# Block products' weights that begin 144 instead of 192 bytes behind their tile's begin

## The chip, the core and the metric

One core of one Trainium2 chip runs the whole kernel, one decoder layer over 512 tokens, in one launch. The metric is device time in microseconds. Before the change three runs took 1109.86, 1110.81 and 1111.26 us, a median of 1110.81 us.

## What is computed

The layer has three stages in a row: a SwiGLU feed-forward network (FFN) at half weight, a token mixer (two kinds of attention), and a second FFN at half weight. Each is normalised before and after. Only the FFNs are touched here. Cut to what matters:

```python
def swiglu(x, w_gate, w_up, w_down):
    return (jax.nn.silu(x @ w_gate) * (x @ w_up)) @ w_down

h = rms_norm(x, ffn1_pre[l])
x = x + 0.5 * rms_norm(swiglu(h, ffn1_w_gate[l], ffn1_w_up[l], ffn1_w_down[l]), ffn1_post[l])
# token mixer
h = rms_norm(x, ffn2_pre[l])
x = x + 0.5 * rms_norm(swiglu(h, ffn2_w_gate[l], ffn2_w_up[l], ffn2_w_down[l]), ffn2_post[l])
```

`x` is 512 by 1024, `w_gate` and `w_up` are 1024 by 2816, `w_down` is 2816 by 1024, all float32.

## The kernel before

**Precision.** Every float32 operand is split into a high and a low part of type `float32r`: ACT casts the high part (`split`, L384), DVE subtracts it from the source for the low part (L391). A product is then three matmuls (`mm3`): high weights by high data (L413), high weights by low data (L414), low weights by high data (L415). In the profile's rows the moving operand stands first and the weights second: `pb_S<-xh_t,whi` streams `xh_t` past the weights `whi`. The weights of a matmul are loaded by an LDWEIGHTS of its own (PEld in the profile), which runs while the matmul before it streams.

**Weight tiles.** `wpair` takes a pair of tiles, `whi` and `wlo`, each 1088 elements (4352 bytes) in every partition, from a pool of three each. A weight block uses 1024 of them; the argument `shift` says how many elements behind the tile's begin they start. Only `block`, in `ffn`, gives a shift, namely `SHIFT`; all other callers leave it at 0.

**Block products.** Both FFNs take their gate and up products for pairs of 128-column groups by a Strassen scheme, `strassen(p)`: for the first FFN with p from 2 to 10, for the second with p from 1 to 10, so 19 times. One call builds seven weight blocks with `block`, from loaded weights (`raw`) or from DVE sums of them (`tmp_t`), and calls `product` seven times. A `product` is 2 column groups by 4 slices of the contraction by 3 matmuls, 24 matmuls. So there are 7 x 24 = 168 matmuls in a call and 19 x 168 = 3192 in the kernel: 1512 in the first FFN and 1680 in the second. Each has weights of 128 by 128 and a moving operand of 128 by 256: a half of `xh`/`xl` or one of the precomputed token sums in `NN`, `N`, `PT` and `CB` tiles.

**Other products.** The first groups of each FFN (`classical`) and the projections of the mixer use unshifted weight tiles. Those with 256 moving columns are the nearest kin of the block products: the matmuls just ahead of the second FFN's first block product stream the same `xh_t` and `xl_t`, 256 columns, past weights that begin at their tile's begin.

**Addresses.** In the built program all these tiles begin at a byte address that leaves 32 when divided by 128: `whi` and `wlo` at 80800, 85152, 89504, 93856, 98208 and 102560, `xh_t` at 34208, `xl_t` at 50592, and so on. A weight slice of a block begins a multiple of 512 bytes behind its block's begin, a moving slice of 256 columns a multiple of 1024 bytes behind its tile's begin. So, counted within stretches of 128 bytes, every moving operand of these products begins at byte 32, unshifted weights at byte 32, and the block products' weights at byte 96 (32 + 192 = 224 = 128 + 96).

**Order.** The order of the instructions on PE, ACT and DVE is written out in a table (`ORDER`). Neither the order nor a single operation depends on `SHIFT`.

Of the kernel before, what the change touches and what calls it, by code (L numbers as in the profile page):

```python
# [294 lines left out]
            8: ["of"] * 2 + ["V"] * 2, 9: ["KB"] * 4}  # L295
STEPS = (2, 2, 2), (4, 2)
EARLY = 5
SHIFT = 48
HOLD_TAGS = ["W"] * 2 + ["Q"] * 4 + ["KA"] * 2 + ["V"] * 2 + ["CB", "ring"]
PS_BUFS = dict(S=3, T=2, V=1, F=2)  # L300
PS_TAGS = [t for t in PS_BUFS for _ in range(PS_BUFS[t])]
# [7 lines left out]
class Layer:  # L309
# [264 lines left out]
    def ffn(self, n, wg, wu, wd, post, finish, xsrc, tags, nps, aside=None):  # L574
# [37 lines left out]
        def block(src):  # L612

            return self.wsplit(src, [4, 2 * P], None, SHIFT)

# [1294 lines left out]
```

## Time and profile before

| what | us |
|---|---|
| median of three runs | 1110.81 |
| the profiled execution's own time | 1109.86 |
| its span, first to last instruction | 1107.8 |
| around the span | 2.06 |
| first FFN's block products on PE, 59.40 to 237.47 | 178.07 |
| second FFN's block products on PE, 799.12 to 996.54 | 197.42 |

All rows come from one profiled execution. A matmul row's duration covers its whole way through the array, so neighbouring matmuls overlap and the busy time of PE says little about its rate; how fast the array works is seen from the distance between the starts of matmuls that follow each other. The timeline shows those starts to 0.01 us, and over a long stretch the distance comes out to a fraction of a nanosecond.

### The profile page before, as it was taken

The numbers are of one execution on the slowest core, as the hardware profiler recorded it, in microseconds if no ns is written. First come the engines' busy times: TensorE is split into PE (matmuls) and PEld (weight loads), VectorE is DVE, ScalarE is ACT, GpSimd is POOL, SyncE is SP. The second block draws the span as 40 slices with busy tenths as digits, with TensorE's granted clock in tenths as the row PEclk, the third lists the DMA queues.
The fourth block names the chain that finished last, engine by engine and source line by source line (L and its number), as shares of the span: only waits on it lengthen the run. The fifth ranks groups of instructions, "written<-read, shape, count | busy, mean of one in ns | idle before, by whom it ended". The sixth has DMA issues, their size and how long they took to land.

```text
span 1107.8 us, 18832 instructions
## 1 busy us (share of the span) xinstructions
PE 1098.6 (99%) x7070; PEld 996.2 (90%) x7070; DVE 915.5 (83%) x1569; ACT 654.2 (59%) x1185; POOL 79.1 (7%) x112
## 2 busy tenths in 40 slices
PE   9999999999999999999999999999999999999997
PEld 7899999998889988888888998888999999998886
DVE  7799999988787878987666687977898888979674
ACT  6455555566564778787565625645565555558562
POOL 1000000000012022443000000001000000000001
PEclk9999999999999999999999999999999999999999
DMA  9967775788964562202567768683324434267862
GB/s 293 308 199 245 225 228 181 222 289 281 317 203 119 165 168 86 84 22 62 169 217 252 236 181 294 220 292 105 103 89 129 129 122 130 92 196 232 294 221 83
DMA packets 153951, 207.36 MB, mean 187 GB/s; under 512 B 19938, under 2 KB 98562, under 8 KB 153604
## 3 DMA queue, kind: packets, MB, share of 16 engines
q1 hardware_dynamic: 153856, 206.16, 57.5%
q8 instruction: 55, 0.90, 0.3%
q14 instruction: 36, 0.29, 0.1%
q10 hardware_dynamic: 4, 0.00, 0.0%
HBM read 166.76 MB, written 39.37 MB: 186 GB/s over the span
## 4 chain that ended last, share of the span: by engine, by line
PE 92%; DVE 3%; DMA 2%; ACT 1%; issue 1%; POOL 0%; SPq 0%; DVEq 0%; POOLq 0%; ACTq 0%
PE pb_F L413 12%; PE pb_F L415 12%; PE pb_F L414 11%; PE pb_S L415 8%; PE pb_S L413 8%; PE pb_S L414 8%; PE pb_T L415 6%; PE pb_T L413 6%; PE pb_T L414 6%; PE pb_V L413 3%; PE pb_V L415 3%; PE pb_V L414 3%; PE pb_V L1344 2%; PE pb_T L1329 2%; PE pb_S L1063 1%; PE pb_S L1064 1%
## 5 line engine op out<-in xcount | busy, mean ns | idle before, releaser
L384 ACT CAST whi<-raw 128x1024 fp32r<-128x1024 f32 (+1 forms) x213 | 217.5, 1023 | 238.2 <-issue 70.2
L391 DVE TENSOR_TENSOR wlo<-raw,whi 128x1024 fp32r<-128x1024 f32 (+1 forms) x213 | 252.5, 1188 | 91.5 <-ACT whi L384 87.2
L413 PE MATMUL pb_F<-xh_t,whi 128*128 128x512 f32 (+1 forms) x392 | 141.7, 363 | 0.1
L415 PE MATMUL pb_F<-xh_t,wlo 128*128 128x512 f32 (+1 forms) x392 | 140.9, 362 | 0.2 <-DVE wlo L391 0.2
L414 PE MATMUL pb_F<-xl_t,whi 128*128 128x512 f32 (+1 forms) x392 | 140.5, 360 | 0.0
L384 ACT CAST whi<-tmp_t 128x1024 fp32r<-128x1024 f32 x58 | 60.8, 1049 | 55.9 <-PE pb_S L414 22.2
L391 DVE TENSOR_TENSOR wlo<-tmp_t,whi 128x1024 fp32r<-128x1024 f32 x58 | 70.9, 1222 | 16.9 <-ACT whi L384 16.6
L415 PEld LDWEIGHTS pb_F<-xh_t,wlo 128*128 128x128 f32 x392 | 73.9, 188 | 9.5 <-DVE wlo L391 0.6
L413 PEld LDWEIGHTS pb_F<-xh_t,whi 128*128 128x128 f32 x392 | 73.9, 188 | 9.5 <-issue 0.3
L414 PEld LDWEIGHTS pb_F<-xl_t,whi 128*128 128x128 f32 x392 | 73.9, 189 | 8.9
L413 PE MATMUL pb_S<-xh_t,whi 128*128 128x256 f32 (+1 forms) x232 | 66.9, 288 | 0.0
L415 PE MATMUL pb_S<-xh_t,wlo 128*128 128x256 f32 (+1 forms) x232 | 66.7, 288 | 0.0
L414 PE MATMUL pb_S<-xl_t,whi 128*128 128x256 f32 (+1 forms) x232 | 66.6, 287 | 0.0
L1320 POOL TENSOR_SCALAR SP_s<-SP_s,st_t 128x384 f32<-128x384 f32 (+2 forms) x48 | 49.6, 1051 | 100.0 <-DVE wlo L391 50.5
L435 POOL TENSOR_TENSOR rs_t<-rs_t,mhalf_t 128x1 f32<-128x1 f32 x24 | 15.6, 648 | 532.2 <-DVE rs_t L431 531.7
L413 PE MATMUL pb_T<-xh_t,whi 128*128 128x256 f32 x184 | 51.2, 283 | 0.6 <-DVE xl_t L496 0.6
L415 PE MATMUL pb_T<-xh_t,wlo 128*128 128x256 f32 x184 | 51.6, 283 | 0.0
L414 PE MATMUL pb_T<-xl_t,whi 128*128 128x256 f32 x184 | 51.0, 281 | 0.0
L391 DVE TENSOR_TENSOR PT_s<-pb_T,PT_s 128x512 fp32r<-128x512 f32 (+1 forms) x72 | 39.7, 559 | 6.1 <-ACT PT_s L384 5.4
L1069 DVE CUSTOM_DVE_ANT_0 SP_s<-pb_S,W_s 128x128 f32<-128x128 f32 (+2 forms) x92 | 38.6, 443 | 7.1 <-PE pb_S L1064 4.7
L415 PEld LDWEIGHTS pb_S<-xh_t,wlo 128*128 128x128 f32 x232 | 43.7, 188 | 0.6
L414 PEld LDWEIGHTS pb_S<-xl_t,whi 128*128 128x128 f32 x232 | 43.6, 188 | 0.6
(858 smaller groups left out, 3458.6 us busy)
## 6 DMA issues: line engine op xcount, KB each, us to landing
raw<-in_ffn_w_up_dram SPq DMA_DIRECT2D x40, 512.0 KB, 4.5
raw<-in_ffn_w_gate_dram SPq DMA_DIRECT2D x39, 512.0 KB, 4.9
raw<-in_w_in_dram SPq DMA_DIRECT2D x18, 1024.0 KB, 5.6
raw<-in_ffn_w_down_dram SPq DMA_DIRECT2D x14, 1024.0 KB, 5.7
raw<-tdram SPq DMA_DIRECT2D x14, 1024.0 KB, 5.2
NN_s<-in_ffn_w_down_dram SPq DMA_DIRECT2D x22, 512.0 KB, 4.6
tdram<-NN_s SPq DMA_DIRECT2D x22, 512.0 KB, 3.8
odram<-ring_s SPq DMA_DIRECT2D x38, 128.0 KB, 3.5
```

The lines of the kernel that those rows point to most:

```text
L384: self.last_cast = self.nc.scalar.copy(dsthi, src).ins
L391: self.last_rest = self.nc.vector.tensor_sub(dstlo, src, dsthi.bitcast(F32)).ins
L413: mm(out, lhi, rhi, start=start, stop=False, skip_group_check=skip)
L414: mm(out, lhi, rlo, start=False, stop=False, skip_group_check=skip)
L415: mm(out, llo, rhi, start=False, stop=stop, skip_group_check=skip)
L435: nc.gpsimd.tensor_tensor(out=r, in0=v, in1=self.mhalf, op=OP.pow)
L1063: mm(out, q[:, qc], ka[:, kc], start=True, stop=False)
L1064: mm(out, q[:, qc], kb[half][:, kc], start=False, stop=True)
L1069: nc.vector.tensor_tensor_reduce(p, s, w, -1.0, FLOOR, OP.add, OP.min, st_m)
L1320: nc.gpsimd.tensor_scalar(pp, pp, st[:, 1, t:t + 1], None, op0=OP.mult)
L1329: nc.tensor.transpose(b[:, o + (t - kk) * P:o + (t - kk + 1) * P], pt[pn][:, po + kk * P:po + (kk + 1) * P], self.ident)
L1344: self.nc.tensor.matmul(out[:, kk * P:S], v, pp, start=first and kk == 0 and pi == 0, stop=False, skip_group_check=True)
```

## The change

One constant is changed.

```diff
@@ -295,7 +295,7 @@
 STEPS = (2, 2, 2), (4, 2)
 EARLY = 5
-SHIFT = 48
+SHIFT = 36
 HOLD_TAGS = ["W"] * 2 + ["Q"] * 4 + ["KA"] * 2 + ["V"] * 2 + ["CB", "ring"]
```

It is used in one place, L614, and reaches the tiles in `wpair`:

```python
        def block(src):
            return self.wsplit(src, [4, 2 * P], None, SHIFT)
...
            w = self.tile(self.pool, [P, 1088], F32R, tag, tag, 3)[:, shift:shift + n]
```

The high and the low part of each of the 133 weight blocks (19 x 7) now begin 36 elements, 144 bytes, behind the tile's begin. ACT writes the high part there, DVE reads it and writes the low part there, and LDWEIGHTS reads both from there. Within stretches of 128 bytes the block products' weights now begin at byte 48 (32 + 144 = 176 = 128 + 48) instead of byte 96. The tiles, their addresses and sizes, the DMAs, the waits and the order of instructions on each engine stay as they were.

## The prediction

> **What bounds the kernel now.** The page comes first, then PE's waits, then the starts of the matmuls in the block products. From the page:
>
> ```profile
> span 1107.8 us, 18832 instructions
> PE 1098.6 (99%) x7070; PEld 996.2 (90%) x7070; DVE 915.5 (83%) x1569; ACT 654.2 (59%) x1185; POOL 79.1 (7%) x112
> PEclk9999999999999999999999999999999999999999
> PE 92%; DVE 3%; DMA 2%; ACT 1%; issue 1%; POOL 0%; SPq 0%; DVEq 0%; POOLq 0%; ACTq 0%
> ```
>
> PE is busy from end to end at full granted clock, and the chain that ended last is 92% PE. The whole list of PE's waits says the same:
>
> ```profile
> PE pb_V L1798 <- POOL ident_t masks.py:199: 1.5, 1, 1.5
> PE pb_T L413 <- DVE xl_t L496: 0.6, 2, 0.4
> PE pb_S L489 <- DVE tmp_t L484: 0.4, 1, 0.4
> PE pb_F L415 <- DVE wlo L391: 0.2, 1, 0.2
> ```
>
> 2.7 us in all, hardly any in the FFNs. So the time is the number of matmuls by the distance between their starts. Nothing changes the number; the question is whether the address changes the distance. The timeline of PE gives it. Here are the first block product of each FFN and the first matmul behind the last one:
>
> ```profile
> 59.40 0.28 PE L413 MATMUL pb_T<-xh_t,whi 128*128 128x256 f32 x1
> ...
> 237.47 0.40 PE L413 MATMUL pb_F<-whi,Q_s 128*128 128x512 f32 x1
> ...
> 799.12 0.28 PE L413 MATMUL pb_V<-xh_t,whi 128*128 128x256 f32 x1
> ...
> 996.54 0.40 PE L413 MATMUL pb_F<-whi,Q_s 128*128 128x512 f32 x1
> ```
>
> The first FFN's 1512 block matmuls take 237.47 - 59.40 = 178.07 us, 117.8 ns each. The second's 1680 take 996.54 - 799.12 = 197.42 us, 117.5 ns each. Together they are 375.49 us, a third of the kernel.
>
> **Does the address matter at all?** The end of the unshifted matmuls ahead of the second FFN's block products, and the first of these, answer it:
>
> ```profile
> 798.04 0.28 PE L413 MATMUL pb_S<-xh_t,SP_s 128*128 128x256 f32 x1
> 798.16 0.28 PE L414 MATMUL pb_S<-xl_t,SP_s 128*128 128x256 f32 x1
> ...
> 799.00 0.28 PE L415 MATMUL pb_S<-xh_t,SP_s 128*128 128x256 f32 x1
> 799.12 0.28 PE L413 MATMUL pb_V<-xh_t,whi 128*128 128x256 f32 x1
> 799.23 0.28 PE L414 MATMUL pb_V<-xl_t,whi 128*128 128x256 f32 x1
> ...
> 800.14 0.28 PE L413 MATMUL pb_V<-xh_t,whi 128*128 128x256 f32 x1
> ```
>
> The same operands stream, 256 columns each, past weights of the same shape. From 798.04 to 799.12 are 9 steps, 120.0 ns each; from 799.12 to 800.14 also 9 steps, 113.3 ns each. The only thing that differs is where the weights lie: unshifted (byte 32 of a 128-byte stretch, where the moving operand begins as well) against shifted by 192 bytes (byte 96). Later in the same FFN the distance is a third value:
>
> ```profile
> 900.08 0.28 PE L413 MATMUL pb_S<-xh_t,whi 128*128 128x256 f32 x1
> ...
> 903.61 0.28 PE L413 MATMUL pb_F<-NN_s,whi 128*128 128x256 f32 x1
> ```
>
> 30 matmuls in 3.53 us, 117.7 ns. So the very same shift gives 113.3 ns in one stretch and 117.7 in another. The slower rhythm began behind one hold-up, where two starts lie 0.23 us apart, and stayed:
>
> ```profile
> 813.40 0.28 PE L413 MATMUL pb_T<-PT_s,whi 128*128 128x256 f32 x1
> 813.52 0.39 PE L414 MATMUL pb_T<-CB_s,whi 128*128 128x256 f32 x1
> 813.75 0.28 PE L415 MATMUL pb_T<-PT_s,wlo 128*128 128x256 f32 x1
> ```
>
> The weight loads carry the mark too, in the groups by form of two windows, 60 to 236 us (block products, shifted) and 788 to 798 us (unshifted):
>
> ```profile
> L414 PEld LDWEIGHTS pb_T<-xl_t,whi 128*128 128x128 f32 x78 | 14.7, 188 | 0.0
> ...
> L414 PEld LDWEIGHTS pb_T<-xl_t,whi 128*128 128x128 f32 x12 | 2.3, 192 | 0.0
> ```
>
> An unshifted load takes 192 ns, a shifted one 188. I read this as two streams, moving operand and next weights, that start nearly together and get in each other's way when they begin in the same part of the address space. One loss is 120.0 - 113.3 = 6.7 ns: unshifted weights pay it at every matmul, and at 117.8 ns two in three pay it (113.3 + 2/3 x 6.7 = 117.8). That last step is inference: it explains three numbers with one price.
>
> **The change, part by part.**
>
> *Removed, added, moved:* no instruction, DMA or wait. What can move are the durations of the ACT casts and DVE subtractions that write or read the shifted tiles, and the matmuls' distance.
>
> *ACT and DVE.* The groups by form of the first FFN's block products (60 to 236 us) and of a stage with unshifted tiles (240 to 340 us), DVE's two rows first:
>
> ```profile
> L391 DVE TENSOR_TENSOR wlo<-raw,whi 128x1024 fp32r<-128x1024 f32 x35 | 42.6, 1218 | 2.9 <-ACT whi L384 2.8
> ...
> L391 DVE TENSOR_TENSOR wlo<-raw,whi 128x1024 fp32r<-128x1024 f32 x30 | 36.5, 1222 | 11.4 <-ACT whi L384 11.2
> ...
> L384 ACT CAST whi<-raw 128x1024 fp32r<-128x1024 f32 x36 | 37.9, 1052 | 40.7 <-issue 20.2 <-PE pb_S L414 6.3 <-PE pb_F L414 5.1
> ...
> L384 ACT CAST whi<-raw 128x1024 fp32r<-128x1024 f32 x30 | 31.5, 1053 | 22.6 <-PE pb_F L415 6.3 <-PE pb_S L415 5.7 <-PE pb_V L415 4.0
> ```
>
> Shifted or not, DVE needs 1218 against 1222 ns and ACT 1052 against 1053. I cost both at nothing, with 4 ns either way as the bound. PE's lead hides them, and this cover is thin in the first FFN, as the windows show:
>
> ```profile
> 60.00:236.00 176.00, 176.00 (x1497) 176.00 (x1496) 169.43 (x217) 98.11 (x135) 0.00 (x0) 1.00 0.69 220
> 820.00:996.00 176.00, 176.00 (x1497) 176.00 (x1496) 155.16 (x186) 97.78 (x135) 0.00 (x0) 1.00 0.42 132
> ```
>
> DVE is busy 169.43 of 176 us there. If PE slows, DVE gains air. If PE speeds up by more than 6.6 us in that window, DVE is what is late next.
>
> *Matmul distance.* No row shows weights at byte 48, so the price is bounded from both sides. The best row is 113.3 ns. In the second FFN it would take 1680 x 0.1133 = 190.3 us, 7.1 less than now; in the first, DVE's 6.6 us is the most. The gain is at most 13.7 us. The other end of the rows shown is 120.0 ns: 1512 x 0.1200 - 178.07 = 3.4 us in the first FFN, 1680 x 0.1200 - 197.42 = 4.2 us in the second, a loss of 7.6 us. Beyond it I estimate a second loss of 6.7 ns per matmul, 126.7 ns: 3192 x 0.1267 - 375.49 = 28.9 us.
>
> I take 120.0 ns. If stretches of 128 bytes fall into two halves, moving operands (byte 32) begin in the lower one. Unshifted weights begin there too and pay at every matmul. Weights at byte 96 begin in the upper half and pay sometimes or never. At byte 48 they are back in the lower half, in the position of the row with 120.0 ns. The two known points do not prove the halves; of all simple divisions this one gives both of them with one price.
>
> The sum: 1109.86 + 7.6 = 1117.5 us against the profiled execution's own time, which is the lowest of the three runs. The median is 0.95 us above it, 1118.4 us. I predict 1118.
>
> *A rule against it.* The Trainium skill, "TensorE: Matmul & The Clock Gate", Part 2: What happens when you issue a matmul, says that weights come through a read port of their own, and that loading the next ones takes no read bandwidth from the running matmul. By that rule the distance would not depend on the address, and the sum would be 1109.9. The trace disagrees with it, 120.0 against 113.3 ns where only the weights' place differs.
>
> **The rivals.**
>
> *Faster: a clean rhythm.* The block products hold 113.3 ns in one stretch at the very address that elsewhere gives 117.8, so a start phase decides there. If 48 bytes less puts the weights' steps where they never meet the moving operand's, the good rhythm holds throughout. It decides wherever the two streams' steps, not their halves, set the meeting. For it: the row at 799.12 to 800.14 us. Against it: nothing ties byte 48 to that rhythm. Time: 1109.9 - 13.7 = 1096.2, or 1097 by the median; with half of it, 1104.
>
> *No change.* Only a finer step than 16 bytes counts, or the same rhythm is found again: 117.8 ns stays, 1110 to 1111 us. Against it: 0 and 192 are both multiples of 16 and differ. The Trainium skill, "SBUF — State Buffer", Specifications (TRN2), gives 16-byte cachelines; both offsets are multiples of 16, so by that alone nothing changes, and no row here shows a 16-byte step.
>
> *Slower than forecast: two meetings.* The half in which the weights begin now holds only 16 bytes of a weight row instead of 32, so the load needs its second piece earlier. If the array must then wait twice for each matmul, the distance is 126.7 ns and the time 1139. It is my estimate alone; nothing shows it.
>
> **How the numbers follow.** The forecast, about 120 ns in both FFNs (1113 to 1121), gets 0.48; two meetings or part of them 0.09; no change 0.20; a better rhythm 0.23, of which I put 0.11 below 1100. A measurement of this kernel can tell about 0.2%, 2.2 us, from no change. So: faster 0.23, same 0.20, slower 0.57. The range from 1100 to 1122 leaves out the better half of the faster case and nearly all of the two meetings, 0.2 together. The forecast's own range is 1113 to 1121, since cases of both signs hold much of the chance.
>
> **What would show it.** Right: block matmuls start 120 ns apart in both FFNs (181.4 and 201.6 us from first to last), their weight loads take 192 ns as unshifted ones do, no stretch at 113.3 is left, DVE's share in the first FFN falls, and everything between and behind the block products keeps its length. Wrong: a distance at or below 117.8 ns with loads of 188 ns (the halves are not what counts), new PE waits for `wlo` or `whi` (the address reaches DVE or ACT), or two FFNs with different distances (the start phase counts more than the address).

## The result, and the profile after

The changed kernel takes 1115.03 us (median of four runs, 1114.55 to 1116.26), the kernel before beside it 1110.34 us (four runs, 1108.71 to 1111.26). The ratio is 1.0057, with a 95% interval from 1.0029 to 1.0085: slower by 4.7 us. The profiled execution of the changed kernel took 1115.3 us.

The page of the changed kernel, first its span, the busy time of the engines, the granted clock and the chain that ended last:

```profile
span 1113.2 us, 18832 instructions
...
PE 1104.5 (99%) x7070; PEld 1002.5 (90%) x7070; DVE 915.4 (82%) x1569; ACT 654.0 (59%) x1185; POOL 78.8 (7%) x112
...
PEclk9999999999999999999999999999999999999999
...
PE 93%; DVE 3%; DMA 1%; ACT 1%; issue 1%; POOL 0%; SPq 0%; DVEq 0%; POOLq 0%; ACTq 0%
```

The number of instructions is the same, the granted clock is full (0.998 of it on average), and only PE with its weight loads, PEld, is busy for longer (PE 1104.5 against 1098.6 us, PEld 1002.5 against 996.2, the span 5.4 us longer), while DVE and ACT keep theirs. The whole list of PE's waits (total, times, longest, in us) has no new line:

```profile
PE pb_V L1798 <- POOL ident_t masks.py:199: 1.5, 1, 1.5
PE pb_S L489 <- DVE tmp_t L484: 0.5, 2, 0.3
PE pb_F L415 <- DVE wlo L391: 0.2, 1, 0.2
```

So again it is the distance between starts. The timeline, at the same four matmuls as in the prediction (start, duration, then the instruction):

```profile
60.24 0.28 PE L413 MATMUL pb_T<-xh_t,whi 128*128 128x256 f32 x1
...
241.66 0.40 PE L413 MATMUL pb_F<-whi,Q_s 128*128 128x512 f32 x1
...
803.22 0.28 PE L413 MATMUL pb_V<-xh_t,whi 128*128 128x256 f32 x1
...
1002.02 0.39 PE L413 MATMUL pb_F<-whi,Q_s 128*128 128x512 f32 x1
```

| stretch | before, us | after, us | difference |
|---|---|---|---|
| first FFN's block products | 178.07 | 181.42 | +3.35 |
| second FFN's block products | 197.42 | 198.80 | +1.38 |
| between them | 561.65 | 561.56 | -0.09 |
| behind them, to the span's end | 111.26 | 111.18 | -0.08 |
| ahead of them | 59.40 | 60.24 | +0.84 |

The first FFN now runs at 181.42 / 1512 = 120.0 ns, the second at 198.80 / 1680 = 118.3 ns: the same address, two distances. The two block stretches add 4.73 us; the medians differ by 4.69. The 0.84 us ahead of them come before any moved weight is used; in the runs below with the block weights' place alone changed, the first block product starts between 59.2 and 61.2 us.

The weight loads, grouped by form in the window that matches the prediction's (60.84 to 236.84 us, first FFN) and then in the second FFN (806 to 1000 us):

```profile
L414 PEld LDWEIGHTS pb_T<-xl_t,whi 128*128 128x128 f32 x78 | 14.8, 190 | 0.0
...
L414 PEld LDWEIGHTS pb_T<-xl_t,whi 128*128 128x128 f32 x40 | 7.5, 189 | 0.0
```

A load took 188 ns before; it now takes 190 in the first FFN and 189 in the second. DVE's and ACT's rows over the first of these windows, and then the window itself (its length, then the busy time of PE, PEld, DVE, ACT and POOL):

```profile
L391 DVE TENSOR_TENSOR wlo<-raw,whi 128x1024 fp32r<-128x1024 f32 x34 | 41.4, 1217 | 1.5 <-ACT whi L384 1.4
...
L384 ACT CAST whi<-raw 128x1024 fp32r<-128x1024 f32 x35 | 36.7, 1049 | 42.0 <-issue 27.7 <-PE pb_S L414 6.6 <-PE pb_F L414 5.3
```

```profile
60.84:236.84 176.00, 176.00 (x1469) 176.00 (x1468) 166.51 (x213) 96.61 (x133) 0.00 (x0) 1.00 0.67 215
```

Their durations did not move (1218 and 1052 ns before). In 176 us PE fits 1469 matmuls instead of 1497, and DVE is busy 166.51 us instead of 169.43. ACT and DVE also write to the moved places, but their writing does not set the distance. From 140 us on, the trace, which holds starts to 1 ns, has 120 distances in a row of exactly 120 ns, while ACT and DVE write such tiles only part of that time (ACT stands idle for 1.00 us before 146.41 us).

### The profile page after: what moved, and what is told of

It is laid out like the page before. It is cut to its first block, busy times and chain, and to the rows that moved or that the text cites. A ratio compares the mean times of both kernels' runs of the same rounds, so it can differ in the third digit from the quotient of the medians.

```text
span 1113.2 us, 18832 instructions
## 1 busy us (share of the span) xinstructions
PE 1104.5 (99%) x7070; PEld 1002.5 (90%) x7070; DVE 915.4 (82%) x1569; ACT 654.0 (59%) x1185; POOL 78.8 (7%) x112
## 4 chain that ended last, share of the span: by engine, by line
PE 93%; DVE 3%; DMA 1%; ACT 1%; issue 1%; POOL 0%; SPq 0%; DVEq 0%; POOLq 0%; ACTq 0%
PE pb_F L413 12%; PE pb_F L415 12%; PE pb_F L414 11%; PE pb_S L415 8%; PE pb_S L413 8%; PE pb_S L414 8%; PE pb_T L415 6%; PE pb_T L414 6%; PE pb_T L413 6%; PE pb_V L413 3%; PE pb_V L414 3%; PE pb_V L415 3%; PE pb_V L1344 2%; PE pb_T L1329 2%; PE pb_S L1063 1%; PE pb_S L1064 1%
## 5 line engine op out<-in xcount | busy, mean ns | idle before, releaser
L413 PE MATMUL pb_F<-xh_t,whi 128*128 128x512 f32 (+1 forms) x392 | 141.9, 363 | 0.1
L414 PE MATMUL pb_F<-xl_t,whi 128*128 128x512 f32 (+1 forms) x392 | 140.7, 361 | 0.0
L413 PEld LDWEIGHTS pb_F<-xh_t,whi 128*128 128x128 f32 x392 | 74.0, 189 | 9.5 <-issue 0.3
L414 PEld LDWEIGHTS pb_F<-xl_t,whi 128*128 128x128 f32 x392 | 74.0, 189 | 8.9
L413 PE MATMUL pb_S<-xh_t,whi 128*128 128x256 f32 (+1 forms) x232 | 67.6, 291 | 0.0
L414 PE MATMUL pb_S<-xl_t,whi 128*128 128x256 f32 (+1 forms) x232 | 67.3, 290 | 0.0
L414 PE MATMUL pb_T<-xl_t,whi 128*128 128x256 f32 x184 | 51.5, 283 | 0.0
L413 PE MATMUL pb_T<-xh_t,whi 128*128 128x256 f32 x184 | 51.5, 285 | 0.0
L414 PEld LDWEIGHTS pb_S<-xl_t,whi 128*128 128x128 f32 x232 | 44.0, 190 | 0.6
L413 PEld LDWEIGHTS pb_S<-xh_t,whi 128*128 128x128 f32 x232 | 44.0, 190 | 0.6
```

The source lines that it names most:

```text
L413: mm(out, lhi, rhi, start=start, stop=False, skip_group_check=skip)
L414: mm(out, lhi, rlo, start=False, stop=False, skip_group_check=skip)
```

## The experiments

The question is what makes the distance: the half of a 128-byte stretch in which the weights begin (**theory H**, the prediction's), pieces of 64 bytes that are cut by the weights' begin (**theory C**), the phase in which PE enters a stretch, which picks one of several rhythms that a place allows (**theory P**), or the distance of the two operands' begins as such (**theory D**). The expectations name four more: **L** (a period of 256 bytes or more), **Q** (in mix: the FFN's own operands decide; in mix4: the address counts beyond 128 bytes), **0** (the place matters for 256 columns only) and **K** (each place has a short cycle of hold-ups of its own). A rhythm is a pattern of distances that repeats, a hold-up one distance that is longer than those around it. s04, s16, mix, mix4, half, sweep and fine are one execution each. A shift is given in elements of 4 bytes; the kernel before has 48, the changed one 36. "Place" is the byte within 128 at which the weights begin, 32 + 4 x shift; the moving operand is at 32.

### The same places, 128 bytes lower (s04, s16)

```diff
-SHIFT = 36
+SHIFT = 4
```

> The block products' weights begin 16 bytes behind the tile's begin: byte 48 of a 128-byte stretch, as in the changed kernel, but 128 bytes lower. Halves of 128 bytes (theory H): the same rhythms as in the changed kernel, 120.0 ns in the first FFN (181.4 us) and about 118.3 in the second (198.8 us), 1115 us. A longer period, 256 bytes or more (theory L): another distance than with 144 bytes, anywhere from 113 to 127 ns. Only what is written 16 bytes finer counts, nothing else: 117.8 as before the change.

It took 1114.23 us. The first block product of each FFN and the matmul behind the last:

```profile
61.15 0.28 PE L413 MATMUL pb_T<-xh_t,whi 128*128 128x256 f32 x1
...
240.07 0.40 PE L413 MATMUL pb_F<-whi,Q_s 128*128 128x512 f32 x1
...
802.13 0.28 PE L413 MATMUL pb_V<-xh_t,whi 128*128 128x256 f32 x1
...
1000.93 0.40 PE L413 MATMUL pb_F<-whi,Q_s 128*128 128x512 f32 x1
```

178.92 and 198.80 us: 118.3 ns in both. Place 48 gives 118.3 ns in three FFNs of four and 120.0 in one.

```diff
-SHIFT = 48
+SHIFT = 16
```

> The block products' weights begin 64 bytes behind the tile's begin: byte 96 of a 128-byte stretch, as before the change, but 128 bytes lower. Theory H (halves of 128 bytes, nothing beyond): the same as before the change, 117.8 ns in the first FFN (178.1 us) and a mixture of 113.3 and 117.8 in the second (197.4 us), 1110 us. Theory L (a period of 256 bytes or more): another distance in at least one FFN, 113 to 120 ns, 1097 to 1118 us.

It took 1110.23 us, beside 1110.16 for the kernel before on the same chip: 178.08 us in the first FFN, and 197.87 us (117.8 ns from end to end, without the 113.3 ns at the start) in the second.

### Every tile 96 bytes higher (pad96)

```diff
-        self.mhalf = self.sbt("mhalf", [P, 1])
+        self.mhalf = self.sbt("mhalf", [P, 25])[:, 0:1]
```

`mhalf` is a small constant that lies ahead of all these tiles; it grows by 96 bytes. Moving operands and unshifted weights now begin at byte 0 of 128, the block weights at byte 64.

> All tiles lie 96 bytes higher, so that moving operands and unshifted weights begin at byte 0 of a 128-byte stretch and the block products' weights (shift 192 bytes, as before) at byte 64. The distance between moving operand and weights is that of before. Only the relative place counts (theory H in its plain form): 117.8 ns or 113.3 in the block products as before, 120.0 and 226.7 ns elsewhere, 1110 us. Streams are read in pieces of 64 bytes and a piece cut at its begin costs a whole step of 6.7 ns (theory C): 256 columns from byte 32 are 17 pieces, 113.3 ns, from byte 0 only 16, so distances fall by up to 6.7 ns per matmul, to 107 to 113 ns in the block products and 213 to 220 ns for 512 columns; 7070 matmuls by 6.7 ns are 47 us at most, 1065 to 1100 us.

1109.79 us (ten runs) against 1110.16, ratio 0.9996 with an interval from 0.9987 to 1.0006. The first FFN's ends, and nine steps on either side of the second FFN's first block product:

```profile
60.70 0.28 PE L413 MATMUL pb_T<-xh_t,whi 128*128 128x256 f32 x1
...
238.78 0.40 PE L413 MATMUL pb_F<-whi,Q_s 128*128 128x512 f32 x1
...
799.07 0.28 PE L413 MATMUL pb_S<-xh_t,SP_s 128*128 128x256 f32 x1
...
800.15 0.28 PE L413 MATMUL pb_V<-xh_t,whi 128*128 128x256 f32 x1
...
801.17 0.28 PE L413 MATMUL pb_V<-xh_t,whi 128*128 128x256 f32 x1
```

The distances are those of before, place by place: 117.8 ns in the first FFN, 120.0 for unshifted weights, 113.3 and later 117.8 in the second. Moving both operands by 96 bytes changes nothing that can be measured; what counts is where the weights lie against the moving operand. Theory C falls.

### Two places in turn (mix)

```diff
-            return self.wsplit(src, [4, 2 * P], None, SHIFT)
+            return self.wsplit(src, [4, 2 * P], None, SHIFT - 12 * (self.calls % 2))
...
+            self.calls = p
```

> Strassen calls with an odd number use 144 bytes, those with an even number 192, so that each address is entered many times from the other's rhythm. Theory P (the phase at the entry picks the rhythm): the calls with 144 bytes show at least two distances, 118.3 and 120.0 ns, within one FFN, and the calls with 192 bytes 113.3 and 117.8. Theory Q (the FFN's own operands pick it): 144-byte calls take 120.0 in the first FFN and 118.3 in the second throughout, 192-byte calls 117.8 in the first. Time between 1105 and 1116 us.

1113.52 us. The starts of calls p = 3 and 4 of the first FFN, then of p = 1 to 4 of the second (odd calls have shift 36, even ones 48):

```profile
79.57 0.28 PE L413 MATMUL pb_S<-xh_t,whi 128*128 128x256 f32 x1
...
99.73 0.28 PE L413 MATMUL pb_T<-xh_t,whi 128*128 128x256 f32 x1
...
800.73 0.28 PE L413 MATMUL pb_V<-xh_t,whi 128*128 128x256 f32 x1
...
820.61 0.28 PE L413 MATMUL pb_S<-xh_t,whi 128*128 128x256 f32 x1
...
840.40 0.29 PE L413 MATMUL pb_V<-xh_t,whi 128*128 128x256 f32 x1
...
860.56 0.28 PE L413 MATMUL pb_S<-xh_t,whi 128*128 128x256 f32 x1
```

A call is 168 matmuls. The call from 79.57 to 99.73 takes 120.0 ns each, the one from 840.40 to 860.56 the same; the first call of the second FFN, 800.73 to 820.61, takes 118.3, at the same shift. All calls at shift 48 take 117.8. The second FFN shows both distances, so its own operands do not pick one (mix's theory Q falls). So one place has two rhythms, and in this kernel and the changed one alike the faster is found where PE comes from the unshifted 256-column products ahead of the second FFN, the slower at every other entry. That is the pattern of the changed kernel.

### The same, 128 bytes lower (mix4)

```diff
-            return self.wsplit(src, [4, 2 * P], None, SHIFT - 12 * (self.calls % 2))
+            return self.wsplit(src, [4, 2 * P], None, SHIFT - 44 * (self.calls % 2))
```

> As in mix (calls in turn), but the odd calls' weights begin 16 bytes behind the tile's begin instead of 144: the same byte 48 of a piece of 128, 128 bytes lower; the even calls stay at 192 bytes. In mix eight of nine such calls, each entered from a call at 192 bytes in the rhythm of 117.78 ns, ran at 119.97. Theory P (the entry picks one of the two rhythms of byte 48; 128 bytes make no difference): again 119.97 ns in the odd calls, the whole 1113.5 us. Theory Q (the address counts beyond 128 bytes; 16 bytes gave 118.33 ns at all four entries so far, 144 bytes gave 120.0 at nine and 118.33 at two): 118.33 in all the odd calls, the whole 1111.5 to 1112 us.

1111.22 us. The same two kinds of entry as in mix, p = 3 of the first FFN and p = 1 of the second:

```profile
78.97 0.28 PE L413 MATMUL pb_S<-xh_t,whi 128*128 128x256 f32 x1
...
98.86 0.28 PE L413 MATMUL pb_T<-xh_t,whi 128*128 128x256 f32 x1
...
799.54 0.28 PE L413 MATMUL pb_V<-xh_t,whi 128*128 128x256 f32 x1
...
819.42 0.28 PE L413 MATMUL pb_S<-xh_t,whi 128*128 128x256 f32 x1
```

19.89 and 19.88 us, 118.4 and 118.3 ns, and so in all nine odd calls. Shift 4 has now given 118.3 or 118.4 ns at 13 entries of 13 (two in s04, two in the sweep below, nine here); shift 36, at the same byte of 128, 120.0 at nine of eleven. Theory Q of mix4 holds: the place within 128 bytes does not say it all, and the slower rhythm came only with 128 bytes more. Theory P alone expected 119.97 ns here and failed.

### Only one part of the weights moved (half)

```diff
-            w = self.tile(self.pool, [P, 1088], F32R, tag, tag, 3)[:, shift:shift + n]
+            w = self.tile(self.pool, [P, 1088], F32R, tag, tag, 3)[:, shift - shift // 48 * 12 * (tag == "wlo"):][:, :n]
```

> The block products' upper part of the weights (whi) stays 192 bytes behind the tile's begin, the lower part (wlo) goes to 144 bytes. Of each three matmuls two load whi and one wlo. If the loss belongs to a load (a load from the moving operand's half costs its own matmul): 117.8 ns plus a third of the difference, 118.5 ns in the first FFN (179.2 us) and 118.0 to 118.5 in the second. If one load in the wrong half sets the rhythm of all three: 118.3 or 120.0 ns as in the kernel after. If the two-in-three of the losses at 117.8 ns are the two whi loads, a single wlo load in the wrong half may add the third: 120.0 ns.

1110.39 us: 178.08 and 197.87 us, 117.8 ns throughout. With `wlo` at 144 and `whi` at 192 bytes nothing is lost in the first FFN; a price per load, which would have given 118.5 ns, is refuted. `whi` alone wasn't tried.

### A place for every call (sweep, fine)

```diff
-            return self.wsplit(src, [4, 2 * P], None, SHIFT)
+            return self.wsplit(src, [4, 2 * P], None, SWEEP[n][self.calls - 2 + n])
```

> Every Strassen call gets a shift of its own, in elements of 4 bytes: first FFN 48, 4, 8, 12, 16, 20, 24, 28, 32; second FFN 28, 24, 20, 16, 12, 8, 4, 0, 2, 1 (the weights then begin at byte 32 + 4 x shift of a piece of 128 bytes; the moving operand begins at byte 32). Read: the mean distance between starts of block matmuls in each call. Theory H (halves of 128 bytes: weights in the moving operand's half 120.0 or 118.33 ns, in the other half 117.78 or 113.33 ns): shifts 0, 1, 2, 4, 24, 28, 32 give 118.3 to 120.0 ns, shifts 8, 12, 16, 20, 48 give 113.3 to 117.8 ns. Theory D (only the distance between the two starts counts, not halves): a smooth or stepwise change with the shift, symmetric about shift 16, for example 117.8 ns only at 16 and 48 and slower ones at 8 and 20. Theory P (the rhythm found at the entry is kept while it exists): a call that follows a slow call shows the slower of its two rhythms, and the same shift met in rising and in falling order can differ by 1.67 to 4.4 ns. Whole time between 1108 and 1117 us by H.

The run took 1111.97 us. In this kernel's rows the code stands one line lower (L414 for L413). Three calls in a row, at shifts 12, 16 and 20, can be read from the starts of their first matmuls:

```profile
119.32 0.28 PE L414 MATMUL pb_S<-xh_t,whi 128*128 128x256 f32 x1
...
139.11 0.28 PE L414 MATMUL pb_T<-xh_t,whi 128*128 128x256 f32 x1
...
158.16 0.28 PE L414 MATMUL pb_S<-xh_t,whi 128*128 128x256 f32 x1
...
178.11 0.28 PE L414 MATMUL pb_T<-xh_t,whi 128*128 128x256 f32 x1
```

19.79, 19.05 and 19.95 us: 117.8, 113.4 and 118.8 ns. The second sweep takes the places between, and moves the other pairs that `wsplit` makes too:

```diff
-    def wsplit(self, src, shape, behind=None, shift=0):
+    def wsplit(self, src, shape, behind=None, shift=None):
+        if shift is None:
+            self.pairs = getattr(self, "pairs", -1) + 1
+            shift = CYCLE[self.pairs // 2 % 8]
```

> Places between those of the first sweep. Block products by call, in elements of 4 bytes: first FFN 2, 3, 5, 6, 7, 9, 10, 11, 13; second FFN 2, 14, 15, 17, 18, 19, 22, 12, 16, 16. All other pairs of weights, which the first sweep left at shift 0, take 2, 4, 8, 12, 20, 24, 28, 30 in turn, two pairs each. The first sweep refuted the halves of 128 bytes (shift 8 gave 118.33 ns and not 117.8 or less; shift 20 gave 118.8 to 120.0). Theory K (each place has its own short cycle of hold-ups of 16 TensorE cycles, one or two cycles per place, and the entry picks one): shift 2 again 115.6 ns in both FFNs or one other fixed value; every mean is a fraction of 272 and 288 cycles (113.3 to 120.0 ns); values at neighbouring places jump instead of following a curve. Theory D (the distance between the two starts sets a smooth curve with its least at shift 16): 14, 15, 17 and 18 give 113.3 to 117.8 ns, rising on both sides, and 2 and 3 near 118.5 to 120. For 512 columns (two places known: 544 cycles = 226.7 ns at shift 0, 560 cycles = 233.3 ns at shift 16): by K some place gives 528 cycles, 220.0 ns; by a floor at 544 cycles nothing is under 226.5 ns.

It took 1117.82 us. Both sweeps together, each number worked out in the same way over the 168 matmuls of a call (several numbers: calls at different positions):

```
shift (place): ns between starts
 0 (32) 120.0          8 (64) 118.3 118.3         16 (96) 113.4 113.4 113.3 113.3
 1 (36) 118.3          9 (68) 120.0               17 (100) 118.4
 2 (40) 115.6 x3      10 (72) 119.2               18 (104) 118.3
 3 (44) 116.7         11 (76) 117.8               19 (108) 113.4
 4 (48) 118.4 118.3   12 (80) 117.8 117.8 117.8   20 (112) 118.8 120.0
 5 (52) 120.0         13 (84) 113.5               22 (120) 113.3
 6 (56) 121.9         14 (88) 117.8               24 (0)  118.7 118.7
 7 (60) 116.7         15 (92) 119.5               28 (16) 120.0 120.0
32 (32) 118.7         48 (96) 117.8
```

Neither half of 128 bytes is fast or slow as a whole: 115.6 and 116.7 ns stand in the lower one, 118.3 to 120.0 in the upper. **Theory H falls**, and D's smooth curve with it, since 15, 16 and 17 give 119.5, 113.3 and 118.4. What holds is a set of steps in the means, in part: with the lowest distance of 113.33 ns and one loss of 6.67 ns, 115.6, 116.7, 117.8, 118.3 and 120.0 are 1/3, 1/2, 2/3, 3/4 and 1 loss per matmul. But 118.7, 118.8, 119.2 and 119.5 (shifts 24 and 32, 20, 10, 15) lie between these, and 121.9 at shift 6 is above one loss. Nor does a mean of 2/3 say that two matmuls in three pay a whole loss. In the kernel before, the trace has 120 distances from 140 us on of 117 ns (40 times), 118 (67) and 119 (13), none near 113.3 or 120. At 118.3 ns in the changed kernel's second FFN they go 115, 120, 118, 120, 115, 121, 117, 120; at shift 3, with a mean of 116.7, about 113 and 120.5 alternate. So theory K's short cycles are shown, and its whole hold-ups of 6.67 ns stand in some of them and not in others. The same shift found different rhythms too: 16 gave 117.8 in s16 and 113.3 here, 20 gave 118.8 and 120.0.

### The other products moved as well (all16)

```diff
-    def wpair(self, shape, shift=0):
+    def wpair(self, shape, shift=16):
...
-    def wsplit(self, src, shape, behind=None, shift=0):
+    def wsplit(self, src, shape, behind=None, shift=16):
```

> Every pair of whi/wlo weights that now begins at the tile's begin (byte 32 of a piece of 128, the moving operand's own place) begins 64 bytes later (byte 96); the block products stay at 192 bytes, as in the kernel before. Theory H: the 256-column products with such weights go from 120.0 to 117.8 ns (about 700 matmuls, -1.5 us) and the 512-column ones from 226.7 ns to 220.0 to 225 ns if the same hold-up of 6.7 ns or a part of it sits in each (about 2000 matmuls): the whole 1095 to 1107 us. Theory 0 (the place matters only for 256 columns, because a 512-column matmul covers the load of the next weights): 512-column matmuls keep 226.7 to 226.9 ns and the whole is 1107.5 to 1110 us. Slower would be 230 ns or more per 512-column matmul, 1115 us and over.

1116.16 us against 1110.23: ratio 1.0057, from 1.0043 to 1.0071. Of the gain that I expected by theory H only the part at 256 columns came: 72 products outside the blocks went from 120.0 ns (358.02 to 366.66 us before) to 117.8 (359.04 to 367.52 us). Nor did theory 0's equality come; the whole is the end named last, the slower one. The same stretches of 512-column matmuls in the kernel before and in this one, the first pair with `whi`/`wlo` as weights (100 matmuls), the second with them as the moving operand (270 matmuls). Before:

```profile
700.95 0.40 PE L413 MATMUL pb_S<-x_s,whi 128*128 128x512 f32 x1
...
723.68 0.39 PE L415 MATMUL pb_V<-CP_s,wlo 128*128 128x512 f32 x1
...
998.60 0.40 PE L414 MATMUL pb_F<-wlo,Q_s 128*128 128x512 f32 x1
...
1059.84 0.39 PE L413 MATMUL pb_F<-whi,KB_s 128*128 128x512 f32 x1
```

and with all pairs 64 bytes further:

```profile
705.57 0.39 PE L413 MATMUL pb_S<-x_s,whi 128*128 128x512 f32 x1
...
728.90 0.40 PE L415 MATMUL pb_V<-CP_s,wlo 128*128 128x512 f32 x1
...
1004.01 0.39 PE L414 MATMUL pb_F<-wlo,Q_s 128*128 128x512 f32 x1
...
1065.82 0.39 PE L413 MATMUL pb_F<-whi,KB_s 128*128 128x512 f32 x1
```

227.3 against 233.3 ns, and 226.8 against 228.9. At 512 columns the place that is good for 256 loses. The second sweep moved these pairs to eight other places. Seven of them took 230 ns or more; the eighth, shift 30 (place 24), took 227.4 and 227.7 ns as the place of weights in stretches of 22 and 20 matmuls (from 726.43 and 731.91 us) and 229.8 in one of 24 (from 618.72 us). So for 512 columns no place seen beats the moving operand's own, and one comes near it.

### Entering by another place (enter)

```diff
-        def block(src):
+        def block(src, shift=SHIFT):
...
-            w = block(a11)
+            w = block(a11, 12)
```

> The kernel before, but the first of the seven block weights of every Strassen call (24 of its 168 matmuls) begins 48 bytes behind the tile's begin instead of 192; the other six stay at 192. In the first sweep both calls at byte 96 that followed one at byte 80 or 112 ran at 113.36 ns over all of their 168 matmuls, while calls at byte 96 that followed one at byte 48 ran at 117.78. If the entry picks the rhythm (theory P): 24 matmuls at 117.78 and 144 at 113.36 in each call, a mean of 114.0 ns: second FFN 191.5 us and first FFN 172.3 us, the whole down by up to 11 us to 1099 us; if VectorE bounds the first FFN (it was busy 96% of it), that one stays above 174 us and the whole is 1100 to 1103. Rival: the 113.36 ns need a whole call at the other place before it, or a quiet start: then 117.78 stays in every call and the whole is 1109 to 1111 us. A loss (118.3 ns or more in the calls, 1112 us and over) would come from two changes of place per call.

1104.42 us (four runs) against 1109.7: ratio 0.9947, from 0.9931 to 0.9964. In the second FFN the first call starts, leaves the other place after 24 matmuls, and ends like this:

```profile
800.07 0.28 PE L413 MATMUL pb_V<-xh_t,whi 128*128 128x256 f32 x1
...
802.91 0.28 PE L413 MATMUL pb_F<-NN_s,whi 128*128 128x256 f32 x1
...
819.24 0.28 PE L413 MATMUL pb_S<-xh_t,whi 128*128 128x256 f32 x1
```

2.84 / 24 = 118.3 ns, then 16.33 / 144 = 113.4 ns, and so on in all ten calls: 191.48 us, 5.94 less than before. In the first FFN the same edit left 117.8 ns in every call (178.09 us). So the entry decides in one FFN, as theory P has it, and the same entry fails in the other; why is open.

### One place for all calls (s22), and the best of each FFN (both)

```diff
-SHIFT = 48
+SHIFT = 22
```

> The kernel before with all block products' weights 88 bytes behind the tile's begin (byte 120 of a piece of 128), a place that ran at 113.34 ns in the one call where the finer sweep had it. If that is the place's only rhythm: second FFN 190.4 us (-7.0); first FFN 171.4 us if TensorE can run that fast there, but VectorE alone is busy 171.5 us in it, so 171.5 to 174 us (-4 to -6.6); the whole 1096 to 1100 us. If the call's entry had chosen it (it followed a call at byte 108 with the same rhythm) and another rhythm of 117.8 to 120.0 ns is found here: 1108 to 1118 us.

1104.95 us (five runs) against 1109.86, ratio 0.9959 from 0.9945 to 0.9972: 174.64 us in the first FFN, as the first case had it but for 0.6 us, and 196.00 us in the second, 116.7 ns, as neither case had it. Place 120, too, has more than one rhythm. In the first FFN 113.3 ns came back behind each hold-up of calls p = 4 to 8 (two starts up to 0.30 us apart); behind the last one, in call 9, 116.7 ns began and stayed.

```diff
-SHIFT = 48
+SHIFT, ENTRY = (22, 48), (22, 12)
...
+        def block(src, shift=SHIFT[n]):
+            return self.wsplit(src, [4, 2 * P], None, shift)
...
+            w = block(a11, ENTRY[n])
```

> Each FFN takes the place that did best in it: the first FFN's block weights 88 bytes behind the tile's begin as in s22, the second FFN's as in enter (the first block weight of each call at 48 bytes, the rest at 192). If the two FFNs are independent: 174.6 us (-3.4) and 191.5 us (-5.9), the whole 9.3 us under the kernel before, 1100 to 1101.5 us. If the first FFN's place changes how the second is entered, the second FFN keeps 117.78 ns (197.9 us) and the whole is 1106 to 1107.5 us.

1100.83 us (six runs, five of them 1099.53 to 1102.23, one 1107.93) against 1110.33: ratio 0.9928, from 0.9908 to 0.9948. This version beats both kernels. Its four marks, a weight load in the first FFN, and the window of the first FFN (its length, then the busy time of PE, PEld, DVE, ACT and POOL):

```profile
59.69 0.28 PE L413 MATMUL pb_T<-xh_t,whi 128*128 128x256 f32 x1
...
233.66 0.40 PE L413 MATMUL pb_F<-whi,Q_s 128*128 128x512 f32 x1
...
794.74 0.28 PE L413 MATMUL pb_V<-xh_t,whi 128*128 128x256 f32 x1
...
986.22 0.40 PE L413 MATMUL pb_F<-whi,Q_s 128*128 128x512 f32 x1
```

```profile
114.52 0.19 PEld L415 LDWEIGHTS pb_S<-xh_t,wlo 128*128 128x128 f32 x1 [0.22 <-DVE wlo L391]
```

```profile
59.69:233.66 173.97, 173.95 (x1513) 172.81 (x1512) 170.63 (x220) 98.84 (x136) 0.00 (x0) 1.00 0.70 225
```

The first FFN takes 173.97 us (-4.10), the second 191.48 (-5.94). DVE is now busy 170.63 of 173.97 us, and the load at 114.52 us waited 0.22 us for its subtraction: there DVE is what is late next, as the prediction's bound on a gain assumed. Why one run took 1107.93 us is not shown, since there is no trace of it; a slower rhythm in one execution would fit.

## Why the prediction was right, and where it was not

- **The time is the number of matmuls by their distance.** Right. Nothing else moved: no new PE wait, the stretches between and behind within 0.1 us, ACT's and DVE's instructions unchanged to 4 ns. DVE's share in the first FFN fell, as said.
- **First FFN, 120.0 ns, +3.4 us.** The number is right, 120.0 ns and +3.35 us, and in part by luck: the reason given for it, the halves, is wrong, and shift 4 in the same half gives 118.3 ns in this FFN.
- **Second FFN, 120.0 ns, +4.2 us.** This is the term of the sum that was mis-sized: it measured 118.3 ns and +1.38 us. The step that failed is "I take 120.0 ns", one distance for one place. The sign to look for, "two FFNs with different distances", is what came. The runs mix and mix4 show that place 48 has two rhythms, 118.3 and 120.0 ns, which of them are in reach depends on 128 bytes more or less, and the entry picks. So the sum was 7.6 us where 4.7 were measured, and 1118 stands 3 us above 1115.03.
- **No stretch at 113.3 ns left.** Right: the second FFN runs at 118.3 ns from its first call on.
- **Loads of 192 ns.** In direction only: 190 and 189 ns.
- **The halves of 128 bytes.** Wrong, although the number drawn from them was right in one FFN. The sweeps show slow and fast places in both halves. That the place against the moving operand is what counts held (pad96).
- **Two in three pay 6.7 ns at 117.8.** The sum fits, the picture does not: the single distances there are 117 to 119 ns, so no matmul pays a whole loss and none goes free. That two reading streams get in each other's way stays an inference; no run shows what the two share.
- **The clean rhythm** (a rival, 1096 to 1104 us) exists, but not at byte 48: s22, enter and both reach 1100.8 to 1105 us, and in the first FFN of `both`, weight loads wait for DVE (five times, 0.8 us in all) while DVE is busy 170.63 of 173.97 us, as the prediction's bound assumed. **No change** fell to the interval. **Two meetings**, 126.7 ns, was seen nowhere as the mean of a call; the longest in the sweeps is 121.9 ns.

What stays open is the mechanism below the rhythms: what makes a loss at all, why 128 bytes matter at place 48, why the same entry finds 113.3 ns in the second FFN and 117.8 in the first, and why 512 columns want another place than 256.

## What to carry to other kernels

Where PE bounds a stretch and runs without waits, measure the distance between matmul starts: if it differs between stretches of one shape, the place of the weights against the moving operand is worth a sweep, and a different place for each call maps them in one run. Then time the chosen place over the whole kernel, since a place that is fast in one call can fall into a slower rhythm in another, and sweep each column count by itself.

## What the runs showed of the hardware

- The mean distance of 256-column float32r matmuls, each with weights of its own, often stands at 113.3 ns or a simple fraction of 6.67 ns above it (115.6, 116.7, 117.8, 118.3, 120.0), but not always (118.7 to 119.5, 121.9), and the single distances need not be whole losses; at 512 columns the means are 226.8, 228.9 and 233.3 ns, a difference of one third and of about one loss. The Trainium skill, "TensorE: Matmul & The Clock Gate", Part 1: The HAM clock gate (the "warmup" mystery), gives 2.4 GHz for the warm clock; by that page 6.67 ns would be an estimated 16 cycles. No run here shows the clock in GHz.
- Such a rhythm holds over a thousand matmuls and more (1680 at 118.3 ns in the changed kernel's second FFN) and outlives a change of operands. It can be left at a hold-up (113.3 to 117.8 ns in the kernel before, behind 813.52 us) or at a change of place (mix); not every hold-up ends it (s22).
- Four bytes can change it: shifts 15, 16 and 17 give 119.5, 113.3 and 118.4 ns.
- The rule on read ports that the prediction weighed, in the Trainium skill's "TensorE: Matmul & The Clock Gate", Part 2: What happens when you issue a matmul, says that loading the next weights takes no read bandwidth from the running matmul. What the prediction drew from it, a distance that does not depend on the address, is refuted: in the sweeps nothing but the place of the weights differs between the block products' calls, and the distance goes from 113.3 to 121.9 ns. Whether read bandwidth is what is lost, no run here shows.
